# Layer norms with accumulating sums and ScalarE squares, the state scaled ahead, and columns outside in two projections

## The chip, the cores and the metric

One core of one Trainium2 chip. The metric is the device time of one execution in microseconds; 2430.36 us is the median of three runs of the kernel before (2428.82 to 2431.28). A lower time is better.

## The reference

Two blocks, one after the other, on a state x of 256 tokens by 1024 features in float32. The first block has a recurrent branch, a sparse attention, a gated feed-forward net and a per-layer embedding, with RMS norms. The second block has two layers; each mixes tokens, then applies a product-key expert layer, and after both of these comes a layer norm. Only those four norms are touched:

```
def _layer_norm(x, g, b):
    mu = jnp.mean(xf, axis=-1, keepdims=True)
    var = jnp.mean(jnp.square(xf - mu), axis=-1, keepdims=True)
    y = (xf - mu) * lax.rsqrt(var + LN_EPS)
    return (y * g + b)
...
        x = _layer_norm(DN_ALPHA * x + y, ln_mix_g[l], ln_mix_b[l])
        f = _peer(x, peer_w_q[l], peer_sub_keys[l], peer_u[l], peer_v[l])
        x = _layer_norm(DN_ALPHA * x + f, ln_ffn_g[l], ln_ffn_b[l])
```

DN_ALPHA is 4 to the power 0.25, called ALPHA in the kernel.

## The kernel before

**Layout.** The state `self.x` lies in SBUF as [128, 2, 1024]: two token halves (`tt`) of 128 tokens on the partitions. A matmul that needs the state as its moving or stationary operand reads `xT`, the transposed state, which `to_T` makes: TensorE transposes four 128x128 blocks into a bank of PSUM (line 263), then `split` (lines 232 and 233) writes a rounded high part on ScalarE and the remainder, the low part, on VectorE. Each projection thus has three matmuls per block: high by high, low by high, high by low (lines 270 to 272, or 300 to 302).

**Weights.** `weight` loads 1 MB by a DMA from SyncE into a `raw` tile, and splits it in two halves by the same `split`: ScalarE makes `hi` (line 232), VectorE `lo` (line 233), four buffers each. All through the program ScalarE and VectorE make weights for the coming matmuls.

**The stages.** First block; then layer 0 of the second block: `layer_a`, its output projection (`dense_a`), norm 1, expert layer `peer(0)`, norm 2; then layer 1: `layer_b`, its output projection, norm 3, `peer(1)`, norm 4, which writes the output. The norms are called inner (1 to 3) where another stage follows, and the fourth is last.

**Before a norm.** A projection accumulates in four banks of PSUM, `acc[tt][nh]`: token half by column half (512 columns). The matmuls are issued by `wide_a`: token half outermost, then the weight tile `j`, then the column half `nh`, then the blocks `k` of the contraction. In `dense_a` each weight tile holds one column half, so its loop over `nh` has one turn. At the end of `peer` two weight tiles of both column halves remain, the last two of 64 expert pairs; there `j` and `nh` both have two turns. At the end of the feed-forward net there is one tile.

**The norm** (`layer_norm`, line 426) runs, per token half: for each column half a scaled sum on VectorE (line 435, x becomes ALPHA x + acc) and its statistics (436); their aggregate (438), which gives mean and variance; on ScalarE the square root of the variance plus epsilon (440); on VectorE centring times the gain for each column half (441, 448), the reciprocal (444), and the final scaling plus bias (450). After that the output DMA (452) or the transposes and splits by `to_T`.

**The order of work.** Each engine works through its queue in order. The order within the queues is made ahead of time by a planner, which takes instructions as their operands come ready by its own reckoning, the most urgent first; urgency is the place in the program, moved ahead by an offset: 1500 places for the norms (`@urgent`), 350 for weights (`AHEAD`). So the transposes of token half 0 can stand between the last matmuls of a projection, and weight splits of the next stage between the steps of a norm. All waits between engines follow from the operands.

**Tables.** `self.table(AF.Sqrt)` loads ScalarE's table for the square root ahead of each norm. The RMS norms of the first block (`rstd`, line 364) use a square with accumulation and a square root under the same table.

Of the kernel before, what the change touches and what calls it, by code (L numbers as in the profile page):

```python
# [13 lines left out]
AF = mybir.ActivationFunctionType  # L14
ALU = mybir.AluOpType
# [3 lines left out]
S, D = 256, 1024  # L19
# [7 lines left out]
ALPHA = 4.0 ** 0.25  # L27
# [146 lines left out]
class Net:  # L174
# [29 lines left out]
    def acc(self):  # L204
        return self.ps("acc")
# [111 lines left out]
    def wide_a(self, acc, ws, xT, k0, nk, first, final=True):  # L317
        per = nk // 2
        width = ws[0][0][0].shape[1] // per
        for tt in range(2):  # L320
            t = slice(tt * 128, tt * 128 + 128)
            for j, w in enumerate(ws):
                for nh in range(width // 512):
                    for k in range(nk):
                        c0 = (k % per) * width + nh * 512
                        last = final and k == nk - 1 and (width == 512 or j == len(ws) - 1)
                        self.step_a(acc(j, tt, nh), w[k // per], slice(c0, c0 + 512), xT(j), k0 + k, t,
                                    first and k == 0, last)
# [96 lines left out]
    @urgent  # L425
    def layer_norm(self, acc, gb, xT=None, out=None):
        nc = self.nc
        gv, bv = gb
        half = [slice(nh * 512, nh * 512 + 512) for nh in range(2)]
        for tt in range(2):  # L430
            x = self.x[:, tt, :]
            st = self.col("bn", 12).rearrange("p (a b) -> p a b", a=2)
            for nh in range(2):
                c = half[nh]
                nc.vector.scalar_tensor_tensor(x[:, c], x[:, c], ALPHA, acc[tt][nh], op0=ALU.mult, op1=ALU.add)  # L435
                nc.vector.bn_stats(st[:, nh, :], x[:, c])  # L436
            mv = self.col("mv", 2)
            nc.vector.bn_aggr(mv, st)
            sd = self.col("sd")
            nc.scalar.activation(sd, mv[:, 1:2], AF.Sqrt, bias=self.eps5, scale=1.0)  # L440
            nc.vector.scalar_tensor_tensor(x[:, half[0]], x[:, half[0]], mv[:, 0:1], gv[:, half[0]],
                                           op0=ALU.subtract, op1=ALU.mult)
            r = self.col("rstd")
            nc.vector.reciprocal(r, sd)
            for nh in range(2):
                c = half[nh]
                if nh:
                    nc.vector.scalar_tensor_tensor(x[:, c], x[:, c], mv[:, 0:1], gv[:, c],
                                                   op0=ALU.subtract, op1=ALU.mult)
                nc.vector.scalar_tensor_tensor(x[:, c], x[:, c], r, bv[:, c], op0=ALU.mult, op1=ALU.add)  # L450
                if out is not None:
                    nc.sync.dma_start(out[tt * 128:tt * 128 + 128, c], x[:, c])
                if xT is not None:
                    self.to_T(xT, x[:, c], tt, nk=4, k0=4 * nh)

    def load_mem(self):
        self.memT = tuple(self.mp.tile([128, 8, S], F32R, name=f"memT{s}") for s in "hl")
# [425 lines left out]
    def ple(self, xT):  # L883
        nc, io = self.nc, self.io
        bv = self.vec(io["ple_b_gate"])
        acc = self.dense_a(io["w_pleg"], xT)
        xT = self.new_xT()
        self.ple_gate(acc, bv, xT)
        for f in FILL[1]:
            self.fill(f)  # L890
        return xT
# [527 lines left out]
    def run(self):  # L1419
        nc, tc, io = self.nc, self.tc, self.io  # L1420
# [19 lines left out]
        with scope() as stk:  # L1440
            with scope() as banks:
                self.psum(banks, st=2, ms=4, acc=2)
                self.vp = stk.enter_context(tc.tile_pool(reuse_waits="tile", name="vecs", bufs=2))
                self.pp = stk.enter_context(tc.tile_pool(reuse_waits="tile", name="phase", bufs=1))
                mixT = self.layer_a(xT)
            self.psum(stk, st=2, ms=2, acc=4)
            acc, gb = self.dense_a(io["w_out2"][0], mixT, (io["ln_mix_g"][0], io["ln_mix_b"][0]))
            xT = self.new_xT()
            self.layer_norm(acc, gb, xT)
            for f in FILL[3]:  # L1450
                self.fill(f)
            memp.close()
        for l in range(2):
            with scope() as stk:
                self.psum(stk, st=2, ms=2, acc=4)
                self.pp = stk.enter_context(tc.tile_pool(reuse_waits="tile", name="phase", bufs=1))
                acc, gb = self.peer(l, xT)
                self.peer_close.close()
                xT = self.new_xT() if l == 0 else None
                self.layer_norm(acc, gb, xT, self.out if l else None)  # L1460
            if l == 0:
                with scope() as stk:
                    with scope() as banks:
# [5 lines left out]
                    acc, gb = self.dense_a(io["w_out2"][1], mixT, (io["ln_mix_g"][1], io["ln_mix_b"][1]))  # L1469
                    xT = self.new_xT()  # L1470
                    self.layer_norm(acc, gb, xT)


# [15 lines left out]
```

## Time and profile before

| | |
|---|---|
| median of three runs | 2430.36 us (2428.82 to 2431.28) |
| the profiled execution | 2427.0 us |
| its span on the core | 2425.2 us |
| granted TensorE clock, mean | 0.999 of full speed |
| busy: TensorE / VectorE / ScalarE | 2390.2 / 1758.6 / 1221.8 us |
| DMA | 419.95 MB, mean 173 GB/s |

The span runs from the first instruction of the program to the last; the execution's time has some 2 us around it. Busy time is the union of an engine's instructions: consecutive matmuls overlap by design, and their ends are modelled. In the profile's rows PE is TensorE, PEld its weight loads, DVE VectorE, ACT ScalarE, SPq SyncE's queue of DMA issues. A row's tiles are written out<-in.

### The profile page before, as it was taken

What the parts mean: (1) busy time and instruction counts of PE and PEld (TensorE: products, weight loads), DVE (VectorE), ACT (ScalarE), POOL (GpSimd) and SP (SyncE); (2) the same over time, 40 slices, a digit from 0 to 9 for tenths busy, and PEclk for the clock granted to TensorE, in tenths of its full rate; (3) what the DMA queues carried; (4) which work ended last, traced back from release to release, by engine and by line L of the source; (5) the groups of instructions that cost most, each with busy time, mean ns of one, the idle gap of its engine ahead of it and who ended that gap; (6) DMA issues with size and microseconds to landing.
All of it is one profiled execution on the core that took longest, in us unless ns stands there. A gap on an engine that the chain in (4) does not pass through costs nothing.

```text
span 2425.2 us, 43189 instructions
## 1 busy us (share of the span) xinstructions
PE 2390.2 (99%) x17746; PEld 2133.9 (88%) x17746; DVE 1758.6 (73%) x3295; ACT 1221.8 (50%) x1797; POOL 6.7 (0%) x17
## 2 busy tenths in 40 slices
PE   8999999999999999999999999999999999999998
PEld 7988799887899998898888889989999889888887
DVE  5578655565799697697587565669969769758756
ACT  5487544465446534534544445644653454454443
POOL 0000000000000000000000000000000000000000
PEclk9999999999999999999999999999999999999999
DMA  8432555543445544544544554444554454454453
GB/s 305 175 123 101 200 191 185 180 152 128 176 162 187 177 162 166 190 161 172 190 174 168 195 173 178 146 163 166 185 179 163 164 188 163 171 190 174 172 193 139
DMA packets 64551, 419.95 MB, mean 173 GB/s; under 512 B 7664, under 2 KB 10880, under 8 KB 16096
## 3 DMA queue, kind: packets, MB, share of 16 engines
q1 hardware_dynamic: 64352, 417.18, 48.8%
q8 instruction: 139, 2.28, 0.4%
q14 instruction: 60, 0.49, 0.1%
HBM read 416.10 MB, written 1.05 MB: 172 GB/s over the span
## 4 chain that ended last, share of the span: by engine, by line
PE 63%; DVE 2%; issue 0%; ACT 0%; DVEq 0%; ACTq 0%
PE ps_acc L300 10%; PE ps_acc L302 10%; PE ps_acc L301 10%; PE ps_st L270 7%; PE ps_st L271 7%; PE ps_st L272 7%; PE ps_st L292 6%; PE ps_st L293 3%; PE ps_ms L1325 2%; PE ps_ms L1326 2%; DVE lo L233 1%; PE ps_ms L1122 1%; DVE bn L436 0%; PE ps_acc L1221 0%; DVE x L435 0%
## 5 line engine op out<-in xcount | busy, mean ns | idle before, releaser
L233 DVE TENSOR_TENSOR lo<-raw,hi 128x1024 fp32r<-128x1024 f32 (+2 forms) x763 | 924.1, 1214 | 459.3 <-ACT hi L232 450.1
L232 ACT CAST hi<-raw 128x1024 fp32r<-128x1024 f32 (+2 forms) x763 | 792.5, 1041 | 793.6 <-PE ps_st L271 401.9
L270 PE MATMUL ps_st<-xT,hi 128*128 128x256 f32 (+1 forms) x2544 | 727.4, 286 | 0.6 <-DVE H L1299 0.4
L271 PE MATMUL ps_st<-xT,hi 128*128 128x256 f32 (+1 forms) x2544 | 721.8, 284 | 0.0
L272 PE MATMUL ps_st<-xT,lo 128*128 128x256 f32 (+1 forms) x2544 | 720.3, 283 | 0.0
L270 PEld LDWEIGHTS ps_st<-xT,hi 128*128 128x128 f32 (+1 forms) x2544 | 484.1, 190 | 5.3 <-issue 2.5
L271 PEld LDWEIGHTS ps_st<-xT,hi 128*128 128x128 f32 (+1 forms) x2544 | 484.5, 190 | 3.4 <-issue 2.1
L272 PEld LDWEIGHTS ps_st<-xT,lo 128*128 128x128 f32 (+1 forms) x2544 | 484.4, 190 | 2.0 <-issue 1.4
L300 PE MATMUL ps_acc<-hi,ah 128*128 128x512 f32 x1024 | 404.0, 395 | 0.0
L301 PE MATMUL ps_acc<-lo,ah 128*128 128x512 f32 x1024 | 399.1, 390 | 0.0
L302 PE MATMUL ps_acc<-hi,al 128*128 128x512 f32 x1024 | 398.3, 390 | 0.0
L292 PE MATMUL ps_st<-xT,hi 128*128 128x512 f32 x704 | 251.6, 400 | 0.0
L302 PEld LDWEIGHTS ps_acc<-hi,al 128*128 128x128 f32 x1024 | 192.2, 188 | 41.4
L300 PEld LDWEIGHTS ps_acc<-hi,ah 128*128 128x128 f32 x1024 | 192.2, 188 | 39.2 <-ACT ah L232 0.4
L301 PEld LDWEIGHTS ps_acc<-lo,ah 128*128 128x128 f32 x1024 | 192.4, 188 | 37.5
L293 PE MATMUL ps_st<-xT,lo 128*128 128x256 f32 x704 | 197.7, 281 | 0.0
L232 ACT CAST ah<-H 128x512 fp32r<-128x512 f32 x128 | 79.5, 622 | 168.4 <-PE ps_acc L301 168.4
L292 PEld LDWEIGHTS ps_st<-xT,hi 128*128 128x128 f32 x704 | 132.3, 188 | 32.7 <-DVE H L1299 0.6
L233 DVE TENSOR_TENSOR al<-H,ah 128x512 fp32r<-128x512 f32 x128 | 88.4, 692 | 73.8 <-ACT ah L232 73.5
L293 PEld LDWEIGHTS ps_st<-xT,lo 128*128 128x128 f32 x704 | 132.9, 189 | 1.2
L1315 DVE TENSOR_TENSOR oa<-iota,pidx 128x2048 f16<-128x2048 f16 x96 | 116.8, 1217 | 0.0
L1333 DVE SCALAR_TENSOR_TENSOR H<-ps_ms,H 128x256 f32<-128x256 f32 (+2 forms) x224 | 96.5, 456 | 21.4 <-PE ps_ms L1326 21.3
(356 smaller groups left out, 2506.1 us busy)
## 6 DMA issues: line engine op xcount, KB each, us to landing
raw<-in_u SPq DMA_DIRECT2D x128, 1024.0 KB, 4.8
raw<-in_v SPq DMA_DIRECT2D x128, 1024.0 KB, 4.8
raw<-in_w_gu SPq DMA_DIRECT2D x22, 1024.0 KB, 4.8
raw<-in_w_pq SPq DMA_DIRECT2D x16, 1024.0 KB, 4.9
raw<-in_w_out SPq DMA_DIRECT2D x12, 1024.0 KB, 4.8
raw<-in_w_down SPq DMA_DIRECT2D x11, 1024.0 KB, 4.8
raw<-in_b_q SPq DMA_DIRECT2D x9, 1024.0 KB, 4.8
raw<-in_a_vr SPq DMA_DIRECT2D x6, 1024.0 KB, 4.9
```

Of the source, the lines that this page charges most:

```text
L232: self.nc.scalar.copy(hi, src)
L233: self.nc.vector.tensor_sub(lo, src, hi.bitcast(F32))
L270: mm(ps, wh, xh, start=first, stop=False)
L271: mm(ps, wh, xl, start=False, stop=False)
L272: mm(ps, wl, xh, start=False, stop=last)
L292: mm(ps, hi[:, k], xT[2][:, k].rearrange("p s t -> p (s t)"), start=k == 0, stop=False)
L293: mm(ps[:, :S], lo[:, k], xT[0][:, k, :], start=False, stop=k == 7)
L300: mm(ps, xh, w[0][:, c], start=first, stop=False)
L301: mm(ps, xh, w[1][:, c], start=False, stop=False)
L302: mm(ps, xl, w[0][:, c], start=False, stop=last)
L1315: nc.vector.tensor_tensor(out=oa, in0=iot(0, P_KEYS), in1=col(0, P_KEYS), op=ALU.is_equal)
L1333: nc.vector.scalar_tensor_tensor(h, g[:, done:done + n], 1.0 / G_SCALE, h, op0=ALU.mult, op1=ALU.mult)
```

## The change

The norm's sum and statistics are replaced. For each column half one VectorE instruction adds the state to the accumulator and sums its elements along the row, the second starting from the first one's sum; a small one makes the negative mean; ScalarE squares the centred values (the negative mean is its bias), writes them over the accumulators, and sums them; a small VectorE instruction makes the variance. Centring of both column halves stands ahead of the reciprocal in the program. ALPHA is no longer in the sum: a new function `grow` multiplies the state by ALPHA on ScalarE, one instruction per token half, after each of the stages whose state goes into a norm (the gate of the first block, and norms 1 to 3). In `wide_a` the column half is now outside the weight tile.

```diff
--- before.py
+++ after.py
@@ -319,8 +319,8 @@
         width = ws[0][0][0].shape[1] // per
         for tt in range(2):
             t = slice(tt * 128, tt * 128 + 128)
-            for j, w in enumerate(ws):
-                for nh in range(width // 512):
+            for nh in range(width // 512):
+                for j, w in enumerate(ws):
                     for k in range(nk):
                         c0 = (k % per) * width + nh * 512
                         last = final and k == nk - 1 and (width == 512 or j == len(ws) - 1)
@@ -429,29 +429,37 @@
         half = [slice(nh * 512, nh * 512 + 512) for nh in range(2)]
         for tt in range(2):
             x = self.x[:, tt, :]
-            st = self.col("bn", 12).rearrange("p (a b) -> p a b", a=2)
+            sm, ss = self.col("lnsum", 2), self.col("lnsq", 2)
             for nh in range(2):
                 c = half[nh]
-                nc.vector.scalar_tensor_tensor(x[:, c], x[:, c], ALPHA, acc[tt][nh], op0=ALU.mult, op1=ALU.add)
-                nc.vector.bn_stats(st[:, nh, :], x[:, c])
-            mv = self.col("mv", 2)
-            nc.vector.bn_aggr(mv, st)
+                nc.vector.tensor_tensor_reduce(out=x[:, c], in0=acc[tt][nh], in1=x[:, c], scale=1.0,
+                                               scalar=sm[:, 0:1] if nh else 0.0, op0=ALU.add, op1=ALU.add,
+                                               accum_out=sm[:, nh:nh + 1])
+            neg = self.col("lnneg")
+            nc.vector.tensor_scalar(neg, sm[:, 1:2], -1.0 / D, None, op0=ALU.mult)
+            for nh in range(2):
+                nc.scalar.activation(acc[tt][nh], x[:, half[nh]], AF.Square, bias=neg, accum_out=ss[:, nh:nh + 1])
+            var = self.col("lnvar")
+            nc.vector.tensor_scalar(var, ss[:, 0:1], ss[:, 1:2], 1.0 / D, op0=ALU.add, op1=ALU.mult)
             sd = self.col("sd")
-            nc.scalar.activation(sd, mv[:, 1:2], AF.Sqrt, bias=self.eps5, scale=1.0)
-            nc.vector.scalar_tensor_tensor(x[:, half[0]], x[:, half[0]], mv[:, 0:1], gv[:, half[0]],
-                                           op0=ALU.subtract, op1=ALU.mult)
+            nc.scalar.activation(sd, var, AF.Sqrt, bias=self.eps5, scale=1.0)
+            for c in half:
+                nc.vector.scalar_tensor_tensor(x[:, c], x[:, c], neg, gv[:, c], op0=ALU.add, op1=ALU.mult)
             r = self.col("rstd")
             nc.vector.reciprocal(r, sd)
             for nh in range(2):
                 c = half[nh]
-                if nh:
-                    nc.vector.scalar_tensor_tensor(x[:, c], x[:, c], mv[:, 0:1], gv[:, c],
-                                                   op0=ALU.subtract, op1=ALU.mult)
                 nc.vector.scalar_tensor_tensor(x[:, c], x[:, c], r, bv[:, c], op0=ALU.mult, op1=ALU.add)
                 if out is not None:
                     nc.sync.dma_start(out[tt * 128:tt * 128 + 128, c], x[:, c])
                 if xT is not None:
                     self.to_T(xT, x[:, c], tt, nk=4, k0=4 * nh)
+
+    def grow(self):
+
+        for tt in range(2):
+            self.nc.scalar.mul(self.x[:, tt, :], self.x[:, tt, :], ALPHA)
+
 
     def load_mem(self):
         self.memT = tuple(self.mp.tile([128, 8, S], F32R, name=f"memT{s}") for s in "hl")
@@ -886,6 +894,7 @@
         acc = self.dense_a(io["w_pleg"], xT)
         xT = self.new_xT()
         self.ple_gate(acc, bv, xT)
+        self.grow()
         for f in FILL[1]:
             self.fill(f)
         return xT
@@ -1447,6 +1456,7 @@
             acc, gb = self.dense_a(io["w_out2"][0], mixT, (io["ln_mix_g"][0], io["ln_mix_b"][0]))
             xT = self.new_xT()
             self.layer_norm(acc, gb, xT)
+            self.grow()
             for f in FILL[3]:
                 self.fill(f)
             memp.close()
@@ -1458,6 +1468,8 @@
                 self.peer_close.close()
                 xT = self.new_xT() if l == 0 else None
                 self.layer_norm(acc, gb, xT, self.out if l else None)
+                if l == 0:
+                    self.grow()
             if l == 0:
                 with scope() as stk:
                     with scope() as banks:
@@ -1469,6 +1481,7 @@
                     acc, gb = self.dense_a(io["w_out2"][1], mixT, (io["ln_mix_g"][1], io["ln_mix_b"][1]))
                     xT = self.new_xT()
                     self.layer_norm(acc, gb, xT)
+                    self.grow()
 
 
 # ---- launch: one core; inputs and outputs as the reference has them ----
```

## Rows read from the trace of the kernel before

**Rows 1.** Head of the page: the span, and busy time by engine.

```profile
span 2425.2 us, 43189 instructions
...
PE 2390.2 (99%) x17746; PEld 2133.9 (88%) x17746; DVE 1758.6 (73%) x3295; ACT 1221.8 (50%) x1797; POOL 6.7 (0%) x17
```

**Rows 2.** Waits of TensorE: who waited for whom, us in total, times, longest.

```profile
PE ps_acc L301 <- DVE lo L233: 4.2, 5, 1.4
```

**Rows 3.** Busy time by window, behind inner norms; columns as the first line names them.

```profile
core 0: us, PE busy (x) PEld busy (x) DVE busy (x) ACT busy (x) POOL busy (x), PEclk, DMA share, GB/s
626.30:637.50 11.20, 9.18 (x42) 6.03 (x41) 11.20 (x17) 5.18 (x8) 0.00 (x0) 1.00 0.28 97
1448.80:1452.70 3.90, 2.54 (x14) 2.06 (x12) 3.90 (x7) 1.10 (x2) 0.00 (x0) 1.00 0.21 32
1452.70:1456.60 3.90, 3.75 (x13) 3.49 (x13) 3.90 (x8) 0.29 (x1) 0.00 (x0) 0.57 0.85 340
1596.00:1607.00 11.00, 9.00 (x42) 5.98 (x41) 11.00 (x17) 3.89 (x6) 0.00 (x0) 1.00 0.29 96
```

**Rows 4.** Timeline of VectorE at norm 1: start us, duration us, line, op, tiles, idle before.

```profile
622.46 0.69 DVE L435 SCALAR_TENSOR_TENSOR x<-x,ps_acc 128x512 f32<-128x512 f32 x1 [1.30 <-PE ps_acc L302]
...
625.54 1.41 DVE L450 SCALAR_TENSOR_TENSOR x<-x,rstd,raw 128x512 f32<-128x512 f32 x2
626.87 0.68 DVE L435 SCALAR_TENSOR_TENSOR x<-x,ps_acc 128x512 f32<-128x512 f32 x1
627.47 1.22 DVE L233 TENSOR_TENSOR lo<-raw,hi 128x1024 fp32r<-128x1024 f32 x1
628.60 0.69 DVE L436 BATCH_NORM_STATS2 bn<-x 128x6 f32<-128x512 f32 x1
...
632.72 0.20 DVE L438 BATCH_NORM_AGGREGATE mv<-bn 128x2 f32<-128x12 f32 x1
```

**Rows 5.** Timeline of TensorE behind norm 1.

```profile
626.44 1.23 PE L263 MATMUL ps_ms<-ident,x 128*128 128x128 f32 x8
...
629.72 0.50 PE L300 MATMUL ps_acc<-hi,xT 128*128 128x512 f32 x1 [0.68 <-ACT xT L232]
...
632.85 0.50 PE L301 MATMUL ps_acc<-lo,xT 128*128 128x512 f32 x1 [0.89 <-DVE lo L233]
...
636.20 1.29 PE L263 MATMUL ps_ms<-ident,x 128*128 128x128 f32 x8 [0.33 <-DVE x L450]
```

**Rows 6.** VectorE by line and shape: count, busy us, mean ns, idle before.

```profile
L699 DVE CUSTOM_DVE_ANT_0 P<-ps_sc,bias 128x256 f32<-128x256 f32 x32 | 12.0, 418 | 4.2 <-PE ps_sc L694 4.2
...
L699 DVE CUSTOM_DVE_ANT_0 P<-ps_sc,bias 128x128 f32<-128x128 f32 x32 | 7.8, 285 | 2.1 <-PE ps_sc L694 2.0
...
L1123 DVE CUSTOM_DVE_ANT_0 bP<-ps_ms,c_dil,bm 128x256 f32<-128x256 f32 x12 | 5.8, 481 | 0.5 <-PE ps_ms L1122 0.4
...
L699 DVE DVE_READ_ACCUMULATOR2_ANT mneg<- 128x1 f32 x64 | 5.3, 83 | 0.0
```

**Rows 7.** ScalarE by line and shape.

```profile
L704 ACT ACTIVATE P<-P,mneg 128x256 f32<-128x256 f32 x32 | 16.0, 506 | 1.2 <-DVE mneg L699 1.2
...
L704 ACT ACTIVATION_READ_ACCUMULATOR P<-P,mneg 128x1 f32 x64 | 12.4, 194 | 0.0
...
L364 ACT ACTIVATE scr<-x 128x1024 f32<-128x1024 f32 x4 | 4.2, 1054 | 0.2 <-DMA x<-in_x 0.2
...
L774 ACT ACTIVATE ri<-av 128x512 f32<-128x512 f32 x4 | 2.5, 632 | 0.0
```

**Rows 8.** Timeline of all engines at the end of the program.

```profile
2416.87 0.39 PE L302 MATMUL ps_acc<-hi,al 128*128 128x512 f32 x1
...
2417.59 0.67 DVE L435 SCALAR_TENSOR_TENSOR x<-x,ps_acc 128x512 f32<-128x512 f32 x1
...
2419.27 0.29 ACT L440 ACTIVATE sd<-mv,eps 128x1 f32<-128x1 f32 x1 [5.42 <-DVE mv L438]
...
2419.93 0.16 DVE L444 RECIPROCAL rstd<-sd 128x1 f32<-128x1 f32 x1
...
2420.66 1.41 DVE L450 SCALAR_TENSOR_TENSOR x<-x,rstd,raw 128x512 f32<-128x512 f32 x2
```

## The prediction

> **What bounds the kernel now.** The page comes first: a span of 2425.2 us, with TensorE busy for 2390.2 us of it [rows 1]. So no edit to a norm can win more than what TensorE idles around that norm, plus what follows the last matmul. The profiled execution took 2427.0 us, 3.4 us under the median of the three timed runs (2430.36); I work the change out as a difference on this trace and put it on the median.
>
> Next, the waits of TensorE: they are short and scattered, and the kind that bears on this change is a wait for the low part of a weight that VectorE has not yet made, 4.2 us in five places [rows 2]. The windows view then shows where. Behind each of the three inner layer norms lies a stretch in which VectorE is busy throughout: 11.20 of 11.20 us, then 3.90 of 3.90 twice, then 11.00 of 11.00, while TensorE idles 2.02 us (9.18 of 11.20), 1.51 us over two windows (1.36 + 0.15) and 2.00 us (9.00 of 11.00) [rows 3]. In the middle one the granted clock falls to 0.57 (1.2 GHz for most of that window), after TensorE had stood idle 1.36 us of the window before: 13 matmuls take 3.75 us there, against 14 in 2.54 us just before, so 13 would have taken 2.36 us and the fall costs 1.4 us of TensorE time [rows 3]. VectorE is thus the bound after a norm, because the norm of token half 1 shares its queue with the next stage's weight splits (line 233) [rows 4]. TensorE's waits in the first stretch show what it misses: ScalarE's split of the normed state (0.68 us), a weight's low part (0.89 us), the state itself (0.33 us) [rows 5]. The last norm has nothing beside it: the last matmul ends at 2417.26, VectorE's last write at 2422.07, 4.81 us later [rows 8].
>
> **The change, part by part.**
>
> *Residual sum and statistics.* Per token half five entries of VectorE's queue go. In the crowded stretch an entry starts 0.08 us before the one ahead of it ends (626.87 + 0.68 against 627.47); so read, the old ones (sum 0.60, statistics 0.61, each twice, aggregate 0.12 [rows 4]) take 2.54 us. New are two sums with accumulation. A row of this kind has 256 columns: 0.418 us, or 0.481 with the running scalar read from a column [rows 6]. Between 128 columns (0.285) and 256 it grows by 0.133, so 256 more add 0.27: 0.69 and 0.75 us, and with the same overlap 0.61 and 0.67. Two accumulator reads last 0.083 us [rows 6], mostly under their neighbour: 0.04 each. The two [128,1] operations are like the reciprocal, 0.16 us long with the next start after 0.08 [rows 8]: 0.1 each. Sum 1.56 us, so relief of 0.98 us per half. Bounds: 0.6 us if every entry counts in full, 1.3 us if the small ones vanish.
>
> The Trainium skill, VectorE: DVE Perf Modes, section Rules for kernel authors, speaks against this: it tells one to minimize the count of operations, and the count rises from 10 to 11 per half with the accumulator reads. By that rule nothing is relieved (the third rival's time). The rows disagree: an entry of 512 columns costs 0.60 of VectorE's time and a small one 0.1.
>
> *The squares on ScalarE.* No row shows ScalarE writing 512 columns into PSUM. A square of 512 columns between SBUF tiles took 0.632 us without a bias column; an activation of 256 columns with one and with accumulation took 0.506, and 1024 columns cost 0.42 more than 512, so 0.21 more for 256: 0.72 us [rows 7]. I bound it by 0.63 (the bias column is free) and 0.92 (256 columns more cost what 512 did) and take 0.72, nearest to both rows. The read behind it (0.194) overlaps half: 0.09 us past the second square [rows 7].
>
> *Chain of one half*, from the second sum's start (0.03 us for a hand-over is an allowance of mine): sum and its read 0.75; scaling to the negative mean with its hand-over 0.19; 0.03 to ScalarE; squares 1.44; read 0.09; variance with both hops 0.22; square root 0.295 [rows 8] runs beside the second centring (0.65, from 2.65 to 3.30); reciprocal 0.08; two final operations 1.41. Last write at 4.79. If the planner puts both centrings behind the variance, 0.65 more; with squares of 0.63, 0.18 less. Before, from the same point (2417.59) to 2422.07 it was 4.48, but the sum had started 0.33 us after the last matmul, since VectorE was behind [rows 8]. The new sum can start 0.04 after it: 4.83 against 4.81. The tail is level, between -0.2 and +0.8; I take +0.2.
>
> *Token half 0 in the inner norms.* Its first final operation ended 3.82 us after the second sum's start (622.46 to 625.54 + 0.74, two that overlap lasting 1.41) [rows 4]; now 3.38 + 0.74 = 4.12, or 4.8 in the worse order. I take 0.4 us late. The transposes began at 626.44 [rows 5], 0.16 after that end, and after them (627.67) matmuls ran on to the wait that ended at 629.72, that is to 629.04: 1.4 us of reserve. So part of the delay may be hidden; I charge all 0.4.
>
> *Token half 1* sits in the stretch that VectorE fills: its relief of 0.98 counts in full, at the waits for a weight and for the state [rows 5]. Per inner norm -0.98 + 0.4 = -0.58. The middle one also has the wait of 1.36 us before the clock's fall; with that wait shorter the fall may go. Of its 1.4 us half is covered, since the state of half 1 was not there either: -0.7 more.
>
> *Column half outer in the two expert projections* (the swapped loops of wide_a). A matmul of 384 columns took 0.18 us (14 in 2.54 us [rows 3]), so one of 512 about 0.24; the first column half of a token half is now done after 12 of 24 rather than 18, 1.4 us sooner. The second is done when it was, and both the mean and the squares need it, so this moves one sum into idle time: 0 in the tail, at most -0.3 in the middle norm. In the other calls one of the two loops has a single turn: nothing.
>
> *State scaled ahead.* Eight ScalarE instructions of 1024 columns, 1.05 us each [rows 7]; two per norm and two after the gate. They wait for the transposes that read the state; behind them in ScalarE's queue stand weight splits. ScalarE is busy for 5.18 of 11.20 and 3.89 of 11.00 us there [rows 3], and the result is wanted a whole stage later, so I cost them at 0. Without that cover: up to 2.1 us at a place. Removed with it is nothing, for the old multiplication rode in the sum.
>
> *Accumulators held longer.* The squares overwrite them, so a bank comes free some 2.5 us after its sum. The next stage's first banks are those of token half 0, done before token half 1's last matmul, as I read the pools' order: 0. Were it a bank of half 1, TensorE would wait about 2 us there, which the second rival's price covers.
>
> Sum: -0.58 - 0.58 - 1.28 + 0.2 = -2.24 us; 2424.8 us for this execution, 2428.1 us for the median.
>
> **The rivals.**
>
> 1. *The waits close.* Relief comes where the weight splits need it, all three stretches lose their whole idle time (5.5 us), the clock stays up (0.7), and of half 0's delay 0.2 each is left: -5.6 us, 2424.8. For it: every one of these waits ends on VectorE or stands behind it [rows 5]. Against: the relief per half is under 1 us, and a stretch idles 2.
>
> 2. *ScalarE becomes the link that is late* (slower). The squares are put in a queue that also splits weights, 1.05 us each; if two such splits stand ahead of half 1's squares in each inner norm, its state comes 2.0 - 0.98 = 1.0 us late, TensorE waits over 1.3 us where it waited 0.33, and the clock falls in the first and third stretch too (1.4 each, as in the middle one): 3 x 1.0 + 2 x 1.4 + 0.65 in the tail = +6.5, 2436.9. It decides once ScalarE's queue is more than about 1 us behind at that point. For it: ScalarE already kept TensorE 0.68 us from the split state [rows 5]. Against: it is idle over half the stretch [rows 3].
>
> 3. *No relief.* Every new entry needs the one ahead of it, across two engines, and where nothing fills the hole VectorE idles for one square: -0.98 + 0.72 + 0.4 = +0.14 per inner norm, +0.3 in the tail, +0.7 in all, 2431.1. For it: the chain now changes engine four times where it did twice. Against: in the crowded stretch there are weight splits to fill with [rows 4]. The rule in the Trainium skill's VectorE: DVE Perf Modes, Rules for kernel authors, would have it come out this way too.
>
> **How the numbers follow.** A measurement of this kernel tells 0.2%, 4.9 us, from no change: faster is under 2425.5, slower over 2435.2. My forecast has 0.47 (its own range 2426 to 2430.5), the first rival 0.25, the second 0.13, the third 0.15. Faster: most of the first rival (0.19) and an edge of the forecast (0.04): 0.23. Slower: most of the second (0.12). The rest, 0.65, is within. The range runs to 2424.0, which takes in most of the first rival, and to 2434.5, which leaves out the second.
>
> **What would show it.** Right: VectorE has accumulating sums of 0.69 to 0.75 us in place of sums and statistics, squares of about 0.72 us on ScalarE, idle TensorE in the three stretches down by a few tenths to 1 us each, no lower clock in the middle one, and 4.6 to 5.6 us from the last matmul to the last write. Wrong: new TensorE waits for ScalarE (weights or split state) after a norm, a lower clock in the first or third stretch, or scalings of the state that stand before a weight's split while TensorE waits for it. A difference above 5 us that arises away from the norms would mean that the planner's order moved elsewhere, for which nothing here argues.

## The result, and the profile after

The changed kernel takes 2461.87 us (median of 4 runs, 2460.94 to 2462.83) against 2429.86 us of the kernel before on the same chip (2428.82 to 2431.28): a ratio of 1.0135, 95% interval 1.0123 to 1.0147. It is 1.35% slower, some 32 us, where 2428.1 had been forecast; the range ended at 2434.5. The profiled execution took 2462.83 us. Its page begins so, against [rows 1]:

```profile
span 2461.1 us, 43238 instructions
...
PE 2417.0 (98%) x17746; PEld 2146.3 (87%) x17746; DVE 1751.6 (71%) x3303; ACT 1240.4 (50%) x1837; POOL 6.7 (0%) x17
```

The span grew by 35.9 us. TensorE has the same 17746 matmuls, yet is busy for 26.8 us more; only 9.1 us of the growth is TensorE idle. VectorE's busy time fell by 7 us and ScalarE's rose by 18.6.

To see where the time arises, take one event that each kernel has once per stage: the start of a norm's first sum (the first row of line 435 behind a pause of over 50 us, in VectorE's timeline). The spaces between these starts, in the profiled executions of six kernels (e1 to e4 are told below):

| us | before | after | e1 | e2 | e3 | e4 |
|---|---|---|---|---|---|---|
| start to norm 1 | 619.74 | 624.38 | 620.61 | 623.59 | 619.65 | 621.98 |
| norm 1 and expert layer 0 | 821.18 | 834.02 | 825.58 | 828.77 | 820.45 | 820.40 |
| norm 2, token mixing of layer 1 | 148.43 | 153.14 | 153.01 | 148.00 | 149.39 | 147.07 |
| norm 3 and expert layer 1 | 821.15 | 833.40 | 825.72 | 828.90 | 820.56 | 820.12 |
| norm 4 | 14.70 | 16.16 | 15.88 | 14.94 | 15.69 | 15.83 |

One part of the change moves this event itself: with the column half outermost and nothing else (e3), the first sums of norms 2 and 4 start 0.6 to 1.0 us sooner, which only shifts time from one row to the next. So kernels with that part are held against e3. The kernel after loses 13.57 and 12.84 us in the two stretches that hold an expert layer, and 3.75 in the one that holds a norm and no expert layer. Two losses lie in this: one of some 4 to 5 us that comes with each inner norm, and one of some 8 us that comes with each expert layer and has no business there. Of the 4.64 us ahead of any norm some 1.3 are the drift told below; the rest is not explained, and two kernels with the same instructions differ there by 2.1 (619.74 before, 621.85 in e7).

**The norms.** TensorE's waits of the kernel after (who waited for whom, us in total, times, longest), to be held against [rows 2]:

```profile
PE ps_ms L263 <- DVE x L452: 8.7, 5, 5.2
PE ps_acc L300 <- ACT ps_acc L441: 6.5, 2, 3.3
...
PE ps_acc L301 <- DVE lo L233: 1.0, 2, 0.8
```

The wait that the change was to shorten did fall, from 4.2 to 1.0 us. Two others stand above it. The transposes (line 263) wait 8.7 us for the normed state, where in the kernel before it was 0.6:

```profile
PE ps_ms L263 <- DVE x L450: 0.6, 2, 0.3
```

The other is new: the next projection's first matmul waits for ScalarE's squares (line 441) to give a bank back. The timeline of norm 1 shows both (start, duration, engine, line, tiles, idle before):

```profile
627.10 0.75 DVE L435 CUSTOM_DVE_ANT_0 x<-ps_acc,x,lnsum 128x512 f32<-128x512 f32 x1 [2.02 <-PE ps_acc L302]
...
628.08 0.69 ACT L441 ACTIVATE ps_acc<-x,lnneg 128x512 f32<-128x512 f32 x1 [3.85 <-DVE lnneg L439]
...
630.62 1.05 ACT L232 CAST hi<-raw 128x1024 fp32r<-128x1024 f32 x1 [1.01 <-DMA raw<-in_w_pq]
...
631.57 0.29 ACT L445 ACTIVATE sd<-lnvar,eps 128x1 f32<-128x1 f32 x1
...
633.99 1.23 PE L263 MATMUL ps_ms<-ident,x 128*128 128x128 f32 x8 [1.49 <-DVE x L452]
634.42 0.75 DVE L435 CUSTOM_DVE_ANT_0 x<-ps_acc,x,lnsum 128x512 f32<-128x512 f32 x1
...
635.94 1.07 ACT L461 ACTIVATE x<-x 128x1024 f32<-128x1024 f32 x1
...
637.43 0.14 DVE L439 TENSOR_SCALAR lnneg<-lnsum 128x1 f32<-128x1 f32 x1
...
637.61 0.69 ACT L441 ACTIVATE ps_acc<-x,lnneg 128x512 f32<-128x512 f32 x1 [0.60 <-DVE lnneg L439]
...
638.47 0.80 PE L300 MATMUL ps_acc<-hi,xT 128*128 128x512 f32 x1 [3.25 <-ACT ps_acc L441]
```

Read it from the end. The projection's first matmul starts at 638.47, 0.17 us after the first square of token half 1 (637.61 + 0.69), and had waited 3.25 us for it: its bank is one of token half 1. ScalarE had stood idle 0.60 us before that square, waiting for VectorE's negative mean (line 439, 637.43). Further up, the square root of half 0 stands in ScalarE's queue behind a weight split that waits 1.01 us for its DMA. What follows is in the windows of the same kernel (columns as in [rows 3]):

```profile
632.50:636.90 4.40, 1.23 (x9) 0.84 (x8) 4.40 (x8) 4.11 (x6) 0.00 (x0) 1.00 0.01 2
636.90:647.00 10.10, 7.77 (x22) 6.02 (x23) 7.16 (x13) 4.05 (x9) 0.00 (x0) 0.50 0.71 243
...
1475.00:1480.00 5.00, 5.00 (x19) 5.00 (x18) 1.38 (x2) 2.13 (x3) 0.00 (x0) 0.50 0.91 346
```

After 4.4 us in which TensorE was busy for 1.23, it has a granted clock of 0.50 (1.2 GHz) for 10.1 us. Behind norm 2 it is 0.50 over 5 us, where before only one window of 3.9 us stood at 0.57 [rows 3].

**The drift.** TensorE by line and shape (count, busy us, mean ns), first two rows of the kernel before, then the same of the kernel after:

```profile
L301 PE MATMUL ps_acc<-lo,ah 128*128 128x512 f32 x1024 | 399.1, 390 | 0.0
...
L301 PE MATMUL ps_acc<-lo,acth 128*128 128x512 f32 x88 | 34.4, 390 | 0.0
```

```profile
L301 PE MATMUL ps_acc<-lo,ah 128*128 128x512 f32 x1024 | 404.7, 395 | 0.0
...
L301 PE MATMUL ps_acc<-lo,acth 128*128 128x512 f32 x88 | 34.7, 395 | 0.0
...
L301 PEld LDWEIGHTS ps_acc<-lo,ah 128*128 128x128 f32 x1024 | 192.8, 188 | 42.6 <-DVE lo L233 0.6
```

Each 512-column matmul of the expert and down projections lasts 5 ns longer, waiting for nothing (0.0 idle), its weight load unchanged at 188 ns. In the timeline the typical distance from one such start to the next is 227 ns before and 232 after. There are 3072 of them with ah or al as the stationary operand and 264 with acth or actl: 3336 x 5.2 = 17 us. No line of the change touches these instructions.

### The profile page after: what moved, and what is told of

Same layout as the page of the kernel before. It is cut to its first block, busy times and chain, and to the rows that moved or that the text cites. A ratio compares the mean times of both kernels' runs of the same rounds, so it can differ in the third digit from the quotient of the medians.

```text
span 2461.1 us, 43238 instructions
## 1 busy us (share of the span) xinstructions
PE 2417.0 (98%) x17746; PEld 2146.3 (87%) x17746; DVE 1751.6 (71%) x3303; ACT 1240.4 (50%) x1837; POOL 6.7 (0%) x17
## 3 DMA queue, kind: packets, MB, share of 16 engines
HBM read 416.10 MB, written 1.05 MB: 170 GB/s over the span
## 4 chain that ended last, share of the span: by engine, by line
PE 64%; DVE 2%; ACT 0%; issue 0%; DVEq 0%; ACTq 0%
PE ps_acc L300 10%; PE ps_acc L301 10%; PE ps_acc L302 10%; PE ps_st L270 7%; PE ps_st L271 7%; PE ps_st L272 7%; PE ps_st L292 6%; PE ps_st L293 3%; PE ps_ms L1335 2%; PE ps_ms L1334 2%; DVE lo L233 1%; PE ps_ms L1131 1%; PE ps_acc L1230 0%; DVE x L447 0%; PE ps_ms L263 0%; DVE xT L233 0%
## 5 line engine op out<-in xcount | busy, mean ns | idle before, releaser
L301 PE MATMUL ps_acc<-lo,ah 128*128 128x512 f32 x1024 | 404.7, 395 | 0.0
L302 PE MATMUL ps_acc<-hi,al 128*128 128x512 f32 x1024 | 403.6, 395 | 0.0
L300 PE MATMUL ps_acc<-hi,xT 128*128 128x512 f32 (+1 forms) x272 | 110.4, 406 | 10.1 <-ACT ps_acc L441 6.5
```

Of the source, the lines that this page charges most:

```text
L300: mm(ps, xh, w[0][:, c], start=first, stop=False)
L301: mm(ps, xh, w[1][:, c], start=False, stop=False)
L302: mm(ps, xl, w[0][:, c], start=False, stop=last)
```

## The experiments

**What differs beside the instructions.** The kernel's column helper gives each name four copies. The old columns took 4 x 64 bytes (bn) and 4 x 32 (mv), the four new names take 4 x 4 x 32: 128 bytes more in the small pool, and every tile that is allocated behind it (H, acth, actl, ah, al) lies 128 bytes further in each partition. By the program's allocation ah moves from byte 202688 to 202816, that is from 192 to 64 counted in 256; xT, hi and lo are allocated ahead of it and stay at 192. My theory at this point: this place makes the 5 ns, and the held bank makes the norms' 4 to 5 us. Rivals: the drift comes with the moved order; ScalarE's longer chain, not the bank, delays the norms.

**e1: the old place, the new norm.**

```diff
-            sm, ss = self.col("lnsum", 2), self.col("lnsq", 2)
+            st = self.col("bn", 12); sm, ss = st[:, 0:2], st[:, 8:10]
-            neg = self.col("lnneg")
+            mv = self.col("mv", 2); neg = mv[:, 0:1]
-            var = self.col("lnvar")
+            var = mv[:, 1:2]
```

> The changed kernel with its four small statistics in the two tags that the kernel before uses (12 and 2 columns), so the small pool is not 128 bytes longer and every tile allocated behind it lies where it lay before; the instructions are those of the change. Theory 'address': the 512-column matmuls whose weights are ah, al, acth or actl go back from 232 to 227 ns from start to start, the lateness that grows through the two expert stages and the down projections (about 17 us) goes, the stops behind the norms stay: 2445 us. Rival 'order': the drift comes from the moved instructions or their DMAs, which are still there: 232 ns stay and 2462 us.

2442.76 us, ratio to before 1.0061 (1.0044 to 1.0078): 19 us less than the kernel after. The start-to-start time is 227 ns again, and the table shows the extra time in the expert stretches (against e3) down from 13.57 and 12.84 to 5.13 and 5.16, while norm 2's stretch keeps 3.62.

**e2: the new place, the old norm.** Nothing but 128 bytes more in the tile xT; the order of the instructions is that of before.

```diff
-        x = self.xp.tile([128, 8, 2, S], F32R, name="xT", tag="xT")
+        x = self.xp.tile([128, 16 * S + 32], F32R, name="xT", tag="xT")[:, 0:16 * S].rearrange(...)
```

> The kernel before, with 128 bytes more per partition in the tile xT and nothing else, so all tiles allocated behind it lie 128 bytes further, as in the changed kernel; same instructions in the same order. Theory 'address': 227 becomes 232 ns in the projections with ah, al, acth or actl as weights, and 2447 us. Rival 'order': nothing, 2430 us.

2445.90 us, 1.0070 (1.0054 to 1.0087): +17.4 us over the 2428.51 of before, with no change of an instruction. Rows of e2, the second for matmuls whose stationary operand is xT, which did not move (227 ns from start to start, as before; the mean of this row holds waits):

```profile
L301 PE MATMUL ps_acc<-lo,ah 128*128 128x512 f32 x1024 | 404.3, 395 | 0.0
...
L301 PE MATMUL ps_acc<-lo,xT 128*128 128x512 f32 x240 | 94.9, 397 | 2.9 <-DVE lo L233 2.9
...
L301 PE MATMUL ps_acc<-lo,acth 128*128 128x512 f32 x88 | 34.7, 394 | 0.0
```

So the drift is the place of tiles. e1 and e2 also add up: +14.3 (norm) and +17.4 (place) are 31.7 of the 32.0 us.

**e3: the column half outermost in wide_a, alone.**

> The kernel before with the column half outer in the wide projections alone. Prediction's term: nothing, 2429.9 us within 0.5. Rival: this order is part of the drift (another bank at every group of matmuls) and costs some of the 17 us, so 2433 us or more.

```diff
-            for j, w in enumerate(ws):
-                for nh in range(width // 512):
+            for nh in range(width // 512):
+                for j, w in enumerate(ws):
```

2429.04 us, 1.0004 (0.9995 to 1.0014). The prediction's 0 holds.

**e4: e1, and the squares' output, which nobody reads, in a bank of the pool st.**

```diff
-                nc.scalar.activation(acc[tt][nh], x[:, half[nh]], AF.Square, bias=neg, ...)
+                nc.scalar.activation(self.st(), x[:, half[nh]], AF.Square, bias=neg, ...)
```

> The kernel of the first run with the squares' elementwise output (which nobody reads) written to a bank of another pool, so that an accumulator is free once its sum is taken. Theory 'bank': TensorE's waits of 3.25 us at norms 1 and 3 for the squares of token half 1 go, and with them part of the half clock behind: 2445 less 2 x 3.3 and some 2 us, about 2436 us. Rival 'ScalarE late': what is late is the normalized state itself, since the root waits on ScalarE's queue, so the same time is lost a step later: 2442 to 2445 us.

2427.22 us, 0.9993 (0.9983 to 1.0003): 15.5 us less than e1, more than the 9 that I had expected, and the whole of the norms' loss (1.2 of it are won elsewhere, as told in the part on the prediction). ScalarE has the same work in the same amounts (busy for 1240.6 us against 1240.8 in e1), so the rival is out: its chain alone does not make the loss. Waits and windows of e4, over the same stretches behind norms 1 and 2:

```profile
PE ps_ms L263 <- DVE x L452: 2.4, 3, 1.0
...
PE ps_acc L301 <- DVE lo L233: 1.6, 4, 0.8
```

```profile
626.00:642.00 16.00, 13.90 (x64) 9.99 (x63) 14.34 (x25) 11.24 (x21) 0.00 (x0) 1.00 0.47 179
1448.00:1462.00 14.00, 11.78 (x63) 9.30 (x62) 11.88 (x23) 10.37 (x17) 0.00 (x0) 1.00 0.49 166
```

The waits for a bank are gone, and the clock stays at 1.00 behind both norms. One thing moved beside the squares' output: by the programs' allocation, the first bank that the next stage takes behind norms 1 and 3 is one of token half 1 in the kernel after, and one of token half 0 in e4. So e4 shows what a held bank costs, but does not part the two ways out, a dead output elsewhere and a next stage that starts on a bank of half 0; the second alone is in no run.

The surplus over my expectation is mostly norm 2. The kernel after shows no wait for a bank there, but this one (TensorE and ScalarE, timeline):

```profile
1468.65 0.33 PE L300 MATMUL ps_acc<-hi,xT 128*128 128x384 f32 x1
...
1470.02 0.69 ACT L441 ACTIVATE ps_acc<-x,lnneg 128x512 f32<-128x512 f32 x1 [0.76 <-DVE lnneg L439]
...
1474.18 1.94 PE L263 MATMUL ps_ms<-ident,x 128*128 128x128 f32 x8 [5.19 <-DVE x L452]
```

and e4 at the same point:

```profile
1452.84 0.95 DVE L233 TENSOR_TENSOR lo<-raw,hi 128x768 fp32r<-128x768 f32 x1
...
1453.84 0.19 PEld L301 LDWEIGHTS ps_acc<-lo,xT 128*128 128x128 f32 x1 [1.31 <-DVE lo L233]
1453.84 0.45 PE L301 MATMUL ps_acc<-lo,xT 128*128 128x384 f32 x1 [0.99 <-DVE mv L439]
...
1456.75 0.34 PE L302 MATMUL ps_acc<-hi,xT 128*128 128x384 f32 x1
...
1458.04 1.29 PE L263 MATMUL ps_ms<-ident,x 128*128 128x128 f32 x8 [0.95 <-DVE x L452]
```

In e4 matmuls of token half 0 run on from 1453.84 to 1457.09 while half 1 is normed; in the kernel after the transposes of half 1 stand in front of them in TensorE's queue, so it waits 5.19 us. A held bank does not explain this order: the matmuls that were put back add to a sum that had begun in the same bank at 1467.12, before half 1's first square (1470.02). The wait of 0.99 in e4 is not one for a bank either: it ends with the low part of a weight (1452.84 + 0.95), which the row of the weight load names. So that the loss at norm 2 goes with the squares' place is shown; why the planner moves the transposes is open.

**e5: only ah and al moved, by an empty tile of 128 bytes ahead of them.** By the tiles' names, TensorE's 17746 matmuls follow each other in the same order as before.

> The kernel before with an empty tile of 128 bytes ahead of ah and al in their pool: only these two (the expert projections' weights on TensorE) lie 128 bytes further; the activations of the down projections, the ring H and the rest stay. Theory 'the weights' place counts': the matmuls with ah and al go from 227 to 232 ns, those with acth and actl stay at 227, and about 15 of the 17 us come: 2444 us. Rival 'another tile counts' (H, the one-hot tables, or what VectorE writes beside): 227 ns and 2429 us.

2443.16 us, 1.0058 (1.0041 to 1.0074), +14.1 us. Rows of e5:

```profile
L301 PE MATMUL ps_acc<-lo,ah 128*128 128x512 f32 x1024 | 404.2, 395 | 0.0
...
L301 PE MATMUL ps_acc<-lo,acth 128*128 128x512 f32 x88 | 34.4, 390 | 0.0
```

The price goes with the stationary operand that was moved, and with no other tile.

**e6 and e7: e2's edit with 64 and with 256 bytes.**

> The kernel before with 64 bytes more in xT, so that the weights of the 512-column projections lie on a multiple of 512 bytes instead of 64 below one (448). If the price comes from where a 512-byte row of weights lies against a boundary, this place is at least as good as 448: 227 ns or a little less, 2428 us or less. Rival (the price belongs to every place but the old one): 232 ns, 2446 us.

> The kernel before with 256 bytes more in xT: the weights lie at 192 in 512 instead of 448, the same place in 256. xT itself lies at 192 in 512 and is fast (227 ns). So the period is 256 or less, or 192 is good in its own right: 227 ns and 2429 us. Rival (any move costs): 232 ns and 2446 us.

64 bytes: 2444.64 us, 1.0069 (1.0052 to 1.0086). My guess that a multiple of 512 must be a good place was wrong; it is as bad as 128 (typically 233 ns). 256 bytes: 2428.76 us, 1.0000 (0.9990 to 1.0010), 227 ns. So of the shifts tried, only the one by 256 bytes costs nothing.

**e8: e1 without the scaling ahead** (the state then enters the next sum without its factor ALPHA).

> The kernel of the first run (2442.8 us) with the scaling of the state ahead of the next norm left out, so that the state enters the next sum without its factor. Theory 'bank alone': ScalarE's 1.07 us for one token half stands ahead of the squares of token half 1, so TensorE's waits of 3.25 us for these squares shrink by about 1 us each and the rest stays: 2440 to 2441 us. Rival 'the scaling is what holds ScalarE up': with it gone the squares come early enough, both waits go, and 2430 to 2433 us.

2441.19 us, 1.0054 (1.0038 to 1.0071): 1.6 us less than e1, in ranges that overlap (2440.04 to 2443.23 against 2442.37 to 2445.01). The time is the expected one, but its reason is not: TensorE still waits 6.5 us in two places for the squares, and most of the gain lies in norm 2's stretch (151.69 us against e1's 153.01). The scaling stands ahead of the squares at norm 1 (635.94 above), but they wait for VectorE's mean there, and it is no more than a small part of the loss.

**e9: 64 bytes in front of hi and lo, so that streamed and stationary operands all move together.**

```diff
-        self.eps5 = self.cp.tile([128, 1], F32, name="eps5")
+        self.eps5 = self.cp.tile([128, 24], F32, name="eps5")[:, 0:1]
```

> The kernel before with 64 bytes put in front of everything that TensorE reads, so that the streamed weight matrices (hi, lo) and the stationary operands (xT, acth, ah, al) all move from 192 to 0 in 256 and keep their distances to each other. Theory 'distance' (what counts is where the stationary operand lies relative to the streamed one, in 256 bytes): 227 ns and 2429 us. Rival 'place' (192 is good for the stationary operand in itself, 0 is not): 232 ns in all projections, xT's 720 matmuls of 512 columns among them, so 3336 + 720 matmuls by 5 ns = 20 us or more: 2449 us or above.

2428.86 us, 0.9999 (0.9989 to 1.0008): the stationary operands lie at 0 in 256, the bad place of e6, and nothing is lost. So the distance between the two operands fits, and a good or bad place does not.

**e10 (192 bytes in xT) and e12 (e9's 64 bytes, and 192 behind the state x, so that hi and lo move and the rest is back at 192).**

> The kernel before with 192 bytes more in xT: acth, actl, ah and al lie at 128 in 256, hi, lo and xT stay at 192. Theory 'distance': 232 ns in the projections with ah, al, acth and actl, 2446 us. Rival 'place, with a boundary': places in the upper half of 256 are good, 227 ns and 2429 us.

> The kernel before with 64 bytes in front of the streamed weights (hi, lo and their raw tiles now at 0 in 256) and 192 bytes behind the state x, so that xT, acth, ah and al are 256 bytes further and at 192 as before. Theory 'distance': all projections, those with xT too, go to 232 ns, 2449 us or above. Rival 'place' (of the stationary operand): 227 ns, 2429 us.

e10: 2434.80 us, 1.0022 (1.0013 to 1.0032), typically 229 ns: dearer, but less than at 64 or 128, and less than the 232 ns expected. e12 failed both theories: 2411.16 us, 0.9924 (0.9907 to 0.9940), 18 us under the kernel before. Its rows, with the 256-column matmuls whose stationary operand is hi and whose streamed one is xT (284 ns in the kernels so far):

```profile
L271 PE MATMUL ps_st<-xT,hi 128*128 128x256 f32 x2464 | 687.9, 279 | 0.0
...
L300 PE MATMUL ps_acc<-hi,ah 128*128 128x512 f32 x1024 | 406.7, 397 | 0.0
```

The 512-column matmuls are dearer, as the distance of 192 predicts; but the same move put another distance under the 7392 matmuls of 256 columns, which I had not counted, and these went from 120 to 114 ns start to start (means 121.3 and 117.0).

**e11: the changed kernel with its own columns, the squares in the bank of st, and 128 bytes in xT (256 in all).**

> The changed kernel with its own four statistics tiles as they are, the squares' elementwise output in a bank of the other pool, and 128 bytes more in xT, so that the stationary operands lie 256 bytes further than before, at the same place in 256. Theory: it is the place alone and not which tags the statistics share, so this is as fast as the fourth run, 2427 us. Rival: the shared tags matter by themselves, 2444 us.

2427.32 us, 0.9993 (0.9984 to 1.0003), as e4. Sharing the old columns' names had no part in it.

**e13 to e15: the two distances set apart.** The kernel before with bytes in front of hi, behind x and behind xT, so that the 512-column matmuls with ah, al, acth and actl are at distance 0 and the 256-column ones at 64, 128 and 192. Open was whether the two shapes follow one distance each.

> The kernel before with tiles moved so that the stationary minus the streamed operand is 0 in 256 bytes for the 512-column projections with ah, al, acth and actl (as before), and 64 for the 256-column matmuls with hi or lo against xT (as in the twelfth run, where it was 192 for the first). Theory 'each shape has its own distance': the first are back at 227 ns (229 to 230 in the twelfth run), the others stay at 114 to 118 ns against 120: 2411 less 3336 by 2.6 ns, 2402.5 us. Rival (the two go together, by what else moved): 2411 us.

> As the run before it, with 128 for the 256-column matmuls and 0 for the 512-column ones. Theory 'any distance but 0 helps the 256-column matmuls, where two loads of weights come per 512 columns': 116 ns again, about 2403 us. Rival 'it costs as it does at 512 columns' (5 ns at 128): 125 ns, 7392 matmuls by 5 ns more than before, 2466 us.

> As the run before it, with 192 for the 256-column matmuls and 0 for the 512-column ones. Theory 'any distance but 0 helps': 116 ns, about 2403 us. Rival 'it costs as at 512 columns' (2 to 3 ns on average at 192): 122 ns, 2446 us.

2410.58 us (0.9924, 0.9907 to 0.9941), 2426.09 us (0.9989, 0.9980 to 0.9999) and 2419.77 us (0.9963, 0.9949 to 0.9977). One row of each:

```profile
L271 PE MATMUL ps_st<-xT,hi 128*128 128x256 f32 x2464 | 688.8, 280 | 0.0
```

```profile
L271 PE MATMUL ps_st<-xT,hi 128*128 128x256 f32 x2464 | 696.8, 283 | 0.0
```

```profile
L271 PE MATMUL ps_st<-xT,hi 128*128 128x256 f32 x2464 | 692.1, 281 | 0.0
```

The 512-column matmuls with ah are back at 227 ns in all three, so each pair of operands has its own distance. But 2402.5, 2403 and 2403 us were expected; e13 has the time of its rival (2411), though not for the rival's reason. In e14 and e15 the 256-column matmuls cost more than at 64; "any distance but 0" was wrong in size. In e13, against e12, the ah matmuls won 1.5 ns each (2992 distances, 4.5 us), while the mean of the 256-column ones rose by 0.4 ns (7569, 3.0 us) and xT's by 0.6 (0.5 us); why these rose is not settled.

**e16: the changed norm, squares in the bank of st, on e13's layout.**

> The changed kernel with the squares' elementwise output in the other pool's bank, laid out as the first run of this four (0 for the 512-column projections, 64 for the 256-column matmuls). Theory: the norm's part is what it was before (1.3 us, up to 2.2 by the forecast), so 1 to 2 us under that run: 2401 us if that one takes 2402.5. Rival: with the matmuls ahead of the norms shorter, VectorE and ScalarE are later against TensorE and the norm's chain with its ScalarE leg loses: 2 us or more above that run.

2409.83 us, 0.9922 (0.9905 to 0.9938): the lowest median, 19 us under the kernel before and 52 under the kernel after. Against e13 it is 0.75 us less, in ranges that overlap (2408.73 to 2411.50 and 2409.58 to 2412.38), so the timing does not tell the two apart.

## Why the prediction was wrong

- **The step that failed first: "Accumulators held longer".** It said that "the next stage's first banks are those of token half 0" and put 0; its own "were it a bank of half 1, TensorE would wait about 2 us there" came true, at 3.25 us in norms 1 and 3. At norm 2 the next stage's first bank was one of half 0, as predicted. I had read the pools' order and traced no bank from the stage behind back to its last reader. And the price was not one wait: with the moved transposes of norm 2 and the half clock it is 5.13, 3.62 and 5.16 us at the three inner norms (e1 against e3), 14.3 us in all (e1 against before), all of which goes when the squares go elsewhere (e4).
- **The step that was missing: where tiles lie.** The prediction said of a difference away from the norms that it "would mean that the planner's order moved elsewhere, for which nothing here argues". It was 17.4 us, and needs no moved order (e2): the four operand tiles acth, actl, ah and al lay 128 bytes further. No term held the new columns' bytes.
- **The rest of the sum came near by luck.** e4's and e11's medians, 2427.22 and 2427.32, lie next to the forecast 2428.1, and the timing can't tell their gain from nothing (both intervals reach 1.0003). The time was not won where the forecast had it. To see it, take events that the swapped loops leave in place: the first sums of norms 1 and 3, and the end of the last matmul of each expert layer. e4 against before takes 829.14 us for 829.20 from norm 1 to the end of expert layer 0, 138.33 for 140.41 from there to norm 3, and 827.81 for 827.91 from norm 3 to the end of expert layer 1: 0.06, 2.08 and 0.10 us less, where 0.58, 1.28 and 0.58 had been forecast. Of the 2.08, some 1.2 arise over 120 us behind norm 2, at the first matmul of the projection ahead of norm 3. It waits for VectorE in the kernel before (first row) and not in e4 (second row), where by the programs' allocation its bank is another; the norm's work has no part in that.

```profile
1575.41 0.50 PE L300 MATMUL ps_acc<-hi,xT 128*128 128x512 f32 x1 [0.92 <-DVE xT L233]
```

```profile
1575.54 0.48 PE L300 MATMUL ps_acc<-hi,xT 128*128 128x512 f32 x1
```

- **The clock behind norm 2.** The forecast took 0.7 us for the fall of the clock that might go with a shorter wait. It is gone in e4 (0.88 over 1448 to 1462 us before, 1.00 in e4), but also in e7, which has the instructions of before in the same order and the same wait there (1.38 us against 1.36), at 139.94 us against 140.41 for this stretch:

```profile
1450.00:1464.00 14.00, 11.43 (x61) 9.55 (x60) 11.72 (x19) 6.52 (x10) 0.00 (x0) 1.00 0.59 224
```

  So that wait alone does not bring the fall, and about 0.5 of the 2.08 us is no merit of the norm.
- **Token half 0 was mis-sized.** Its first final operation was to end 0.4 us late. In e4 it ends 6.14 us after the second sum's start at norm 1 and 5.88 at norm 3, against 3.82 before: 2.1 to 2.3 us late. Rows of e4 at norm 1:

```profile
624.70 0.75 DVE L435 CUSTOM_DVE_ANT_0 x<-ps_acc,x,bn 128x512 f32<-128x512 f32 x1 [2.02 <-PE ps_acc L302]
...
630.10 1.41 DVE L452 SCALAR_TENSOR_TENSOR x<-x,rstd,raw 128x512 f32<-128x512 f32 x2
```

  TensorE's transposes then wait 0.80 and 0.62 us for it, at the two norms where nothing was won; the chain had been added up without the weight splits that stand in it on both engines. VectorE itself was relieved: it is busy for 7.0 us less in the kernel after, with one entry more per token half. For that time the rule of the Trainium skill (VectorE: DVE Perf Modes, Rules for kernel authors), to minimize the count, does not hold here. TensorE's gain at these norms, 0.06 and 0.10 us, is nearer to nothing than to the forecast.
- **The instructions were sized well.** Rows of the kernel after, VectorE, then ScalarE:

```profile
L435 DVE CUSTOM_DVE_ANT_0 x<-ps_acc,x,lnsum 128x512 f32<-128x512 f32 x8 | 6.0, 748 | 7.5 <-PE ps_acc L302 7.5
L435 DVE CUSTOM_DVE_ANT_0 x<-ps_acc,x 128x512 f32<-128x512 f32 x8 | 5.5, 684 | 1.6 <-PE ps_acc L302 1.6
```

```profile
L441 ACT ACTIVATE ps_acc<-x,lnneg 128x512 f32<-128x512 f32 x16 | 10.9, 682 | 21.1 <-DVE lnneg L439 21.1
L461 ACT ACTIVATE x<-x 128x1024 f32<-128x1024 f32 x8 | 8.5, 1060 | 0.0
```

  Sums of 0.75 and 0.68 us (forecast 0.75 and 0.69), squares of 0.68 (0.72), scalings of 1.06 (1.05).
- **The tail.** From the last matmul's end to the last write it is 4.98 us against 4.81: +0.17, forecast +0.2. Rows of the kernel after, in order of time:

```profile
2452.41 0.39 PE L302 MATMUL ps_acc<-hi,al 128*128 128x512 f32 x1
2452.84 0.75 DVE L435 CUSTOM_DVE_ANT_0 x<-ps_acc,x,lnsum 128x512 f32<-128x512 f32 x1 [0.17 <-PE ps_acc L302]
...
2456.36 1.42 DVE L452 SCALAR_TENSOR_TENSOR x<-x,rstd,raw 128x512 f32<-128x512 f32 x2
```

- **Column half outer and state scaled ahead:** 0 was right for the first (e3); for the second e8 says at most about 1.6 us, and that only while the squares held the bank.
- **The rivals.** The second had the sign and two of the signs to look for (the clock falls in the first and third stretch, scalings ahead of what TensorE waits for), but not the mechanism: ScalarE's queue is as full in e4, and nothing is lost. It also held the bank's price to be covered by its own, 6.5 us for all three norms; it was 14.3. The third had the outcome of norms 1 and 3 once the bank is put right: next to nothing won.

## What to carry to other kernels

Before an output is written over a bank of PSUM "because it is free", find the next owner of that bank in the trace and the last reader that it will have to wait for; a dead output belongs in a bank that nobody is waiting for. An edit that adds or resizes even a small tile moves every tile behind it: compare the addresses of the operands of the most frequent matmuls before and after, and when a loss is spread evenly over matmuls that nobody edited, test it by padding the kernel before, where no instruction changes. When a repaired version lands next to a forecast, check stage by stage, from events that the change does not move, that its time was won where the forecast had it.

## What the runs showed of the hardware

The time of a matmul depended on the distance between its stationary and its streamed operand in SBUF, counted in 256 bytes. Typical (median) time from one start to the next, worked out from the starts of neighbouring matmuls in the traces:

| stationary minus streamed, in 256 | 0 | 64 | 128 | 192 |
|---|---|---|---|---|
| 512 columns, ah or al against hi or lo | 227 ns (before) | 233 (e6) | 232 (e2) | 229 (e10, e12) |
| 512 columns, xT against hi or lo | 227 (before) | 233 (e15) | 232 (e14) | 229 (e13) |
| 256 columns, hi or lo against xT | 120 (before) | 114 (e13) | 119 (e14) | 118 (e15) |

The first two rows agree though different tiles are moved in them, which makes the distance the best account of it; only steps of 64 bytes were tried. The same distance is the cheapest for one shape and the dearest for the other. Why, the runs do not show: weight loads keep their 188 ns, and the matmuls wait for nothing that the profile names. The kernel before had all of these at distance 0, the best of the four for its 3336 matmuls of 512 columns with ah, al, acth or actl, and the worst for its 7392 of 256. Faster matmuls are also not all gain: in e12 TensorE waits for something that it did not wait for before, a ScalarE activation,

```profile
PE ps_st L270 <- ACT H L1303: 6.6, 4, 1.9
```

so of the 32 us that 7569 distances by 4.3 ns would give, 18 were left. This wait and the dearer 512-column matmuls (2992 by 1.5 ns, 4.5 us) make 11 of the missing 14; the rest is open.
